# Sample attention in a hybrid decoder step: groups of four batches with small tiles, in place of pairs of batches with zero-filled queries

## The chip, the cores and the metric

One Trainium2 chip, of which the kernel uses one core. The metric is the device time of one execution in microseconds (us). A core has a tensor engine (TensorE, PE in the profile, its weight loads PEld), VectorE (DVE), ScalarE (ACT), GpSimd (POOL) and SyncE (SP), whose queue issues most DMA transfers. Each engine runs its instructions in the order in which the program emits them, and waits on semaphores of others.

## The reference

The kernel is one layer of a decoder trunk for two groups of requests: one prompt of 1024 tokens, and eight decode batches ("samples") of 8 new tokens each over 4096 past tokens in a paged cache. Per layer:

```python
h = rms_norm(x) * (1 + scale1) + shift1
z = h @ w_in                              # split among three mixers A, B, C
# A: 8 query heads, 2 key heads, 64 wide. Three branches, mixed by gates:
k_cmp, v_cmp = compress(raw keys), compress(raw values)     # 255 blocks of 32 tokens, stride 16
o_cmp, p     = cmp_attention(q, k_cmp, v_cmp)
top_i, ok    = select_blocks(p, ...)                        # 16 blocks of 64 tokens, per key head and token
o_slc        = slc_attention(q, top_i, ok, k_slc, v_slc)
o_win        = window attention over the last 512 tokens
mix_A        = g0 * o_cmp + g1 * o_slc + g2 * o_win
# B: gated convolution, C: pooling
x = x + gate1 * (concat[A, B, C] @ w_out)
x = x + gate2 * SwiGLU(rms_norm(x) * (1 + scale2) + shift2)
```

A query head r = 0..3 of key group g attends with key head g. For a sample batch that makes 4 heads × 8 tokens = 32 rows per key group, and 64 rows for both.

## The kernel before

The program is one long Python function that emits instructions. Its parts are tasks (generators), each of which emits a step and then yields the time from which its next step can run. A rough clock of the engines (`use`), priorities (`spawn`), conditions (`hold`) and lists of free PSUM banks by tag (`bank_of`, `give`) decide which task emits next. What comes out is a fixed order for each engine; nothing is reordered on the chip by these times. All products go through the helper at L135, transposes through L139, evictions through L150 (ACT) and L152 (DVE), so those lines stand for many sources, and tiles tell them apart.

The stages of the profiled execution: the conditioning up to about 110 us, the input projection up to about 380, the attention from 401 to 843, then the output projection and the feed-forward network. In the attention three tasks are interleaved on PE: the prompt's attention (tiles `kh`, `kl`, `qs`, `pt`, `vt`, `vcp`), the compression of the cached raw keys and values of batches 3 to 7 (tile `stream` from `cacheA`), and the sample attention, which this change is about.

The sample attention before works in four pairs of batches. Rows of a PSUM bank are (batch of the pair, key group, head, token) = 2·2·4·8 = 128. All 128 partitions of a key tile hold both key heads, 64 features each, so the query tile `qb` has 64 columns for a batch and zeros where a row's key group isn't the partition's (`sample_setup`, L1065).

- `sample_select` (L1081) runs once a pair, after both batches are compressed: scores against the 255 compressed blocks and the 16 new keys, softmax, the importance of 64-token blocks, the 16 best by two `max` and `match_replace` steps, a bias per block, and the values of these branches.
- `sample_attention` (L1198) then walks nine units a pair, 36 in all. A unit is 512 keys of each of the two batches, eight pages of 128 KB (`unit` or `stream` tiles, key half and value half): eight units of the cache and one of the window. Two products against the unit's keys fill the bank S, one 64-column tile of PE for each batch:

```python
for b2 in range(2):
    self.mm(S[self.rows(b2), 0:512], self.qb[:, 2 * p + b2], kv[:, b2, :, 0:P], True, True)
```

- DVE adds the bias and takes the row's extreme (L1225), ACT exponentiates (L1232).
- `sample_values` (L1238): four transposes of the 128×512 probabilities `e`, an eviction to `spt`, and eight products of 128 columns, four key tiles for two batches:

```python
for t in range(4):
    for b2 in range(2):
        self.mm(o[self.rows(b2), 0:P], pt[:, t * P + 64 * b2:t * P + 64 * b2 + 64],
                kv[:, b2, t, P:2 * P], t == 0, t == 3)
```

The half of the 128 result columns that belongs to the other key group is not used.

- `sample_load` and `sample_fetch` (L1176, L1187) load the next unit as soon as a buffer is free. There are two `unit` buffers, and three `stream` buffers more when all eight batches are compressed. SyncE issues a unit's eight pages one after the other (L488). A unit's scores wait in emission for `u in self.loads and self.u_done >= u - 1`.
- `sample_combine` (L1260) weighs the 12 partial results `part` of a pair by their maxima and sums and stores the mixture, which the output projection loads.

Constants made before (`constants3`, L293 to L328): `m_new` masks the new keys, `sel` picks a row's gates, `hind` its head, `rsum` sums the heads.

Of the kernel before, what the change touches and what calls it, by code (L numbers as in the profile page):

```python
# [7 lines left out]
F32 = mybir.dt.float32  # L8
# [4 lines left out]
OP = mybir.AluOpType  # L13
# [4 lines left out]
P = 128  # L18
# [42 lines left out]
class Kernel:  # L61
# [55 lines left out]
    def bank_of(self, tag):  # L117
        """waits for a bank of the tag"""
# [4 lines left out]
    # ---------------------------------------------------------------- helpers  # L123
# [22 lines left out]
    def evac(self, out, in_, n, ready=None):  # L146
        """PSUM to SBUF on the engine that is free first; the time at which it is there"""
# [7 lines left out]
    def combine(self, out, a, b, op, n, ready=0.0, eng=None):  # L155
        """out = a op b in SBUF on VectorE or GpSimd, by default the one that is done first"""
# [25 lines left out]
    # ---------------------------------------------------------------- constants  # L182
# [60 lines left out]
    def constants3(self, c):  # L243
        nc = self.nc
        with self.pool("ctmp") as tp:
# [9 lines left out]
            # zeros, then the causal triangle; the window's older edge; the compressed blocks that are not over yet  # L255
# [15 lines left out]
            # row index -> token t of a sample row (b2, g, r, t)  # L271
# [7 lines left out]
            # sum over the four heads of a key group  # L279
# [12 lines left out]
            # new tokens: key (b', t') is seen by row (b, t) when b' == b and t' <= t  # L292
            a = tp.tile([P, 4, 64], F32, name="a")  # L293
            for b2 in range(2):
                nc.gpsimd.iota(a[64 * b2:64 * b2 + 64], pattern=[[-16, 4], [1, 64]], base=-8 * b2,
                               channel_multiplier=0, allow_small_or_imprecise_dtypes=True)
            ge = tp.tile([P, 4, 64], F32, name="ge")
            nc.vector.tensor_scalar(ge, a, 0.0, None, op0=OP.is_ge)
            ok = tp.tile([P, 4, 64], F32, name="ok")
            nc.vector.scalar_tensor_tensor(ok, a, tv[:, 0:1], ge, op0=OP.is_le, op1=OP.mult)  # L300
            self.m_new = c.tile([P, 4, 64], F32, name="m_new")
# [9 lines left out]
            # token partition (64 + (b, t)) -> row (b2, g, r, t) of the pair p  # L311
            self.sel = c.tile([P, 4, P], F32, name="sel")
            si = tp.tile([P, 4, 2, 8, 8], F32, name="si")
            for p in range(4):
                nc.gpsimd.iota(si[:, p], pattern=[[-8, 2], [0, 8], [-1, 8]], base=-64 - 16 * p,
                               channel_multiplier=1, allow_small_or_imprecise_dtypes=True)
            nc.vector.tensor_scalar(self.sel.rearrange("a p r -> a (p r)"), si.rearrange("a p b g t -> a (p b g t)"),
                                    0.0, None, op0=OP.is_equal)

            # head of a sample row  # L320
            hi = tp.tile([P, 8], F32, name="hi")
            for b2 in range(2):
                nc.gpsimd.iota(hi[64 * b2:64 * b2 + 64], pattern=[[-8, 8]], base=0, channel_multiplier=1,
                               allow_small_or_imprecise_dtypes=True)
# [1810 lines left out]
```

## Time and profile before

| | us |
|---|---|
| three runs | 1708.04, 1712.49, 1713.70 |
| median | 1712.49 |
| span of the profiled execution | 1707.9 |
| PE busy in it | 1606.5 (94%) |
| DVE, ACT, POOL busy | 1121.0, 821.8, 704.6 |

The span is the time from the first to the last instruction of the one execution that was profiled. That execution has no device time of its own beside its span; the nearest figure is the span's distance of 4.6 us to the runs' median. In the rows of a view, `L135 PE MATMUL bank<-unit,qb 128*64 128x512 f32 x4` is: line, engine, instruction, what is written from which tiles (moving operand, then weights), the tile of PE as rows*columns, the moving operand's partitions × columns, and the number of records. A product of fp32 operands leaves two records, one for each pass.

### The profile page before, as it was taken

What the parts mean: (1) busy time and instruction counts of PE and PEld (TensorE: products, weight loads), DVE (VectorE), ACT (ScalarE), POOL (GpSimd) and SP (SyncE); (2) the same over time, 40 slices, a digit from 0 to 9 for tenths busy, and PEclk for the clock granted to TensorE, in tenths of its full rate; (3) what the DMA queues carried; (4) which work ended last, traced back from release to release, by engine and by line L of the source; (5) the groups of instructions that cost most, each with busy time, mean ns of one, the idle gap of its engine ahead of it and who ended that gap; (6) DMA issues with size and microseconds to landing.
All of it is one profiled execution on the core that took longest, in us unless ns stands there. A gap on an engine that the chain in (4) does not pass through costs nothing.

```text
span 1707.9 us, 35277 instructions
## 1 busy us (share of the span) xinstructions
PE 1606.5 (94%) x12317; PEld 1427.7 (84%) x12317; DVE 1121.0 (66%) x2886; ACT 821.8 (48%) x1892; POOL 704.6 (41%) x812
## 2 busy tenths in 40 slices
PE   6789999997999999999799789999999999899998
PEld 5689999987877566666599779999999998889997
DVE  1491334767556867666599996555555556998887
ACT  1363212326676766766675543332333334655554
POOL 1121000003342322222206486555555555888976
PEclk9899999999999999999999989999999999999999
DMA  9854455425664644540883224225222225744433
GB/s 273 258 180 127 143 141 138 136 75 179 202 193 128 195 141 122 160 131 10 276 253 105 75 72 135 96 96 194 97 96 100 96 96 186 237 128 130 133 82 125
DMA packets 214851, 245.13 MB, mean 144 GB/s; under 512 B 25985, under 2 KB 182850, under 8 KB 214354
## 3 DMA queue, kind: packets, MB, share of 16 engines
q1 hardware_dynamic: 190546, 209.77, 40.1%
q10 hardware_dynamic: 18288, 17.01, 3.2%
q0 software_dynamic: 5840, 16.10, 2.9%
q8 instruction: 98, 1.61, 0.4%
q14 instruction: 79, 0.65, 0.1%
HBM read 202.33 MB, written 44.67 MB: 145 GB/s over the span
## 4 chain that ended last, share of the span: by engine, by line
PE 31%; DVE 9%; issue 4%; DMA 3%; POOL 3%; ACT 1%; ACTq 0%; POOLq 0%; DVEq 0%; SPq 0%
PE bank L135 31%; DVE w_lo L160 2%; DMA w_raw<-in_wup 2%; POOL w_s L160 1%; DVE b_lo L160 1%; DVE g_lo L160 1%; DVE x L1706 1%; DVE d_lo L160 1%; POOL b_t L160 1%; DMA w_raw<-in_wdown 0%; DMA mixc<-mix_d 0%; ACT w_hi L164 0%; DMA x<-x_d 0%; DVE n_ss L160 0%; POOL f_T L160 0%
## 5 line engine op out<-in xcount | busy, mean ns | idle before, releaser
L135 PE MATMUL bank<-b_lo,w_hi 128*128 128x272 f32 x1232 | 355.8, 291 | 2.7 <-DVE b_lo L160 2.5
L135 PE MATMUL bank<-b_hi,w_hi 128*128 128x272 f32 x1232 | 351.6, 292 | 6.9 <-DVE f_v L1512 3.3
L135 PE MATMUL bank<-b_hi,w_lo 128*128 128x272 f32 x1232 | 351.4, 290 | 2.1 <-DVE w_lo L160 2.1
L135 PEld LDWEIGHTS bank<-b_hi,w_hi 128*128 128x128 f32 x1232 | 232.1, 191 | 9.6 <-ACT b_hi L164 4.9
L135 PEld LDWEIGHTS bank<-b_lo,w_hi 128*128 128x128 f32 x1232 | 234.5, 190 | 4.0 <-DVE b_lo L160 3.9
L135 PEld LDWEIGHTS bank<-b_hi,w_lo 128*128 128x128 f32 x1232 | 233.0, 190 | 3.1 <-DVE w_lo L160 2.8
L160 POOL TENSOR_TENSOR w_s<-w_raw 128x512 f32<-128x512 f32 (+1 forms) x122 | 164.2, 1347 | 147.8 <-DVE w_lo L160 134.1
L1011 POOL TENSOR_SCALAR P<-P,st 128x640 f32<-128x640 f32 (+11 forms) x192 | 111.5, 591 | 241.8 <-DVE st L1009 89.5
L164 ACT ACTIVATE w_hi<-w_raw 128x512 fp32r<-128x512 f32 (+2 forms) x130 | 86.5, 676 | 176.5 <-PE bank L135 141.2
L160 DVE TENSOR_TENSOR w_lo<-w_raw,w_hi 128x512 fp32r<-128x512 f32 (+2 forms) x129 | 115.6, 904 | 83.2 <-PE bank L135 47.4
L160 DVE TENSOR_TENSOR w_lo<-w_s,w_hi 128x512 fp32r<-128x512 f32 (+1 forms) x144 | 127.4, 888 | 45.4 <-ACT w_hi L164 38.6
L135 PE MATMUL bank<-stream 128*128 128x128 f32 x1056 | 137.2, 289 | 19.4 <-DMA stream<-in_cacheA 14.5
L135 PEld LDWEIGHTS bank<-stream 128*128 128x128 f32 x1056 | 130.4, 203 | 28.5 <-issue 21.8
L160 POOL TENSOR_TENSOR x<-x,d_m 128x272 f32<-128x272 f32 x144 | 141.1, 1001 | 25.2 <-DVE x L1706 13.1
L164 ACT ACTIVATE w_hi<-w_s 128x512 fp32r<-128x512 f32 (+1 forms) x144 | 89.2, 624 | 113.2 <-PE bank L135 57.1
L135 PE MATMUL bank<-h_hi,w_hi 128*128 128x384 f32 (+1 forms) x384 | 129.4, 337 | 1.0 <-ACT py L826 1.0
L135 PE MATMUL bank<-h_hi,w_lo 128*128 128x384 f32 (+1 forms) x384 | 126.7, 330 | 0.0
L135 PE MATMUL bank<-h_lo,w_hi 128*128 128x384 f32 (+1 forms) x384 | 126.4, 329 | 0.0
L1003 ACT ACTIVATE P<-P,st 128x640 f32<-128x640 f32 (+11 forms) x192 | 113.0, 591 | 13.0 <-DVE st L994 6.5
L135 PE MATMUL bank<-g_hi,w_hi 128*128 128x272 f32 x308 | 92.0, 301 | 13.1 <-DVE x L1706 6.7
L139 PEld LDWEIGHTS bank<-ident,P 128*128 128x128 f32 (+1 forms) x592 | 64.1, 138 | 46.4 <-issue 30.2
L139 PE MATMUL bank<-ident,P 128*128 128x128 f32 (+1 forms) x592 | 95.6, 284 | 2.5 <-DVE pt L152 1.7
(363 smaller groups left out, 4111.0 us busy)
## 6 DMA issues: line engine op xcount, KB each, us to landing
wada<-in_wada SPq DMA_DIRECT2D x96, 256.0 KB, 5.2
stream<-in_cacheA SPq DMA_DIRECT2D x192, 128.0 KB, 3.1
w_raw<-in_wup SPq DMA_DIRECT2D x48, 512.0 KB, 3.9
g_raw<-g_d SPq DMA_DIRECT2D x70, 272.0 KB, 3.1
unit<-in_cacheB SPq DMA_DIRECT2D x136, 128.0 KB, 2.3
stream<-in_cacheB SPq DMA_DIRECT2D x120, 128.0 KB, 2.2
w_raw<-in_wout SPq DMA_DIRECT2D x24, 512.0 KB, 4.5
g_d<-f_T SPq DMA_DIRECT2D x84, 136.0 KB, 1.8
```

The costliest lines, as they stand in the source:

```text
L135: self.nc.tensor.matmul(out, lhsT, rhs, start=start, stop=stop, skip_group_check=chain)
L139: self.nc.tensor.transpose(out, in_, self.ident)
L160: (self.nc.vector if eng == "dve" else self.nc.gpsimd).tensor_tensor(out, a, b, op=op)
L164: self.nc.scalar.activation(hi, src, AF.Copy)
L1003: nc.scalar.activation(Ps, Ps, AF.Exp, scale=-1.0, bias=sy[:, 0:1], accum_out=sy[:, 1:2])
L1011: nc.gpsimd.tensor_scalar(Ps, Ps, sy[:, 3:4], 0.0, op0=OP.mult, op1=OP.add)
L1706: nc.vector.scalar_tensor_tensor(out[:, :n], acc[:, :n], self.mod[:, 5, m, 0:1], out[:, :n], op0=OP.mult, op1=OP.add)
```

## The change

The sample attention works in two groups Q of four batches. Rows of a bank are (batch, head, token) = 4·4·8 = 128 for one key group, and there is a bank, a bias, a probability tile and so on for each of the two key groups. `qb` has 32 columns and no zeros: partitions 0 to 63 hold the queries of key group 0, the others those of group 1. Scores are products of tiles with 64 rows (a key group's features) and 32 columns (a batch's rows), eight for a step at eight places of the PE array. A value product has 32 columns of weights and 64 moving columns (a key group's values alone), four batches at four column places, 32 products a step. A step takes two of the units of before, and there are 18. `sample_select` runs once a group, waits for four batches, and loads keys and values of the blocks as separate halves.

```diff
 def sample_setup(self, pool):
-        self.qb = pool.tile([P, NB, 64], F32, name="qb")
-        nc.vector.memset(self.qb, 0.0)
-        for g in range(2):
-            s = slice(64 * g, 64 * g + 64)
-            nc.vector.tensor_copy(
-                self.qb[s].rearrange("p b (g r t) -> p g b r t", g=2, r=4)[:, g],
-                self.q[s, :, SEQ:].rearrange("p r (b t) -> p b r t", t=NT))
+        self.qb = pool.tile([P, NB, 32], F32, name="qb")
+        nc.vector.tensor_copy(self.qb.rearrange("p b (r t) -> p b r t", r=4),
+                              self.q[:, :, SEQ:].rearrange("p r (b t) -> p b r t", t=NT))
...
-    def rows(self, b2):
-        return slice(64 * b2, 64 * b2 + 64)
+    def rows(self, b):
+        return slice(32 * b, 32 * b + 32)
+    def group(self, g):
+        return slice(64 * g, 64 * g + 64)
+    def sample_scores(self, S, col, Q, keys):
+        for b in range(4):
+            for g in range(2):
+                k = keys(b)[self.group(g)]
+                n = 1
+                for d in k.shape[1:]:
+                    n *= d
+                self.mm(S[g][self.rows(b), col:col + n], self.qb[self.group(g), 4 * Q + b], k, True, True)
...
 def sample_select(self, pool, Q, st):
-        yield from self.hold(lambda: self.cmp_done >= 2 * p + 2)
-        for b2 in range(2):
-            t = pool.tile([P, 2, 256], F32, name="kvc", bufs=2)
-            nc.sync.dma_start(t, self.cmp_d[2 * p + b2])
-            kv.append(t)
+        yield from self.hold(lambda: self.cmp_done >= 4 * Q + 4)
+        def load(x):
+            t = [pool.tile([P, 2, P], F32, name="kvc", bufs=4) for b in range(4)]
+            for b in range(4):
+                nc.sync.dma_start(t[b], self.cmp_d[4 * Q + b][:, :, x * P:(x + 1) * P])
+            return t, self.use("dma", 1.5, self.t["pe"]) + 2.5
+        K, at = load(0)
...
+        self.sample_scores(S, 0, Q, lambda b: K[b])
+        self.sample_scores(S, 256, Q, lambda b: self.kn)
+        V, at = load(1)
+        for g in range(2):
...
+            for h in range(2):
+                n = P if h == 0 else NCMP - P
+                for b in range(4):
+                    self.mm(o[self.rows(b), 0:64], ct[:n, h, self.rows(b)], V[b][:n, h, self.group(g)], h == 0, h == 1)
...
 def sample_fetch(self, u, kv):
-        p, x = divmod(u, 9)
+        Q, x, c = u // 18, u % 18 // 2, u % 2
...
 def sample_attention(self, pool):
-        for u in range(36):
+        for Q in range(2):
+            self.spawn(1, self.sample_select(pool, Q, sts[Q]))
+        for u in range(18):
...
-            yield from self.hold(lambda: "at" in st and u in self.loads and self.u_done >= u - 1)
+            yield from self.hold(lambda: "at" in st and 2 * u + 1 in self.loads and self.u_done >= 2 * u - 2)
+            kv, at, src = zip(*[self.loads.pop(2 * u + c) for c in range(2)])
...
-            S = yield from self.bank_of("S")
-            for b2 in range(2):
-                self.mm(S[self.rows(b2), 0:512], self.qb[:, 2 * p + b2], kv[:, b2, :, 0:P], True, True)
+            S = []
+            for g in range(2):
+                S.append((yield from self.bank_of("S")))
+            self.sample_scores(S, 0, Q, lambda b: kv[b // 2][:, b % 2, :, 0:P])
...
 def sample_values(self, pool, u, st, kv, es, nx, src):
...
-        for t in range(4):
-            for b2 in range(2):
-                self.mm(o[self.rows(b2), 0:P], pt[:, t * P + 64 * b2:t * P + 64 * b2 + 64], kv[:, b2, t, P:2 * P],
-                        t == 0, t == 3)
+        for g in range(2):
+            for t in range(4):
+                for b in range(4):
+                    self.mm(o[self.rows(b), self.group(g)], pts[g][:, t * P + 32 * b:t * P + 32 * b + 32],
+                            kv[b // 2][:, b % 2, t, P + 64 * g:P + 64 * g + 64], t == 0, t == 3)
...
-        self.unit_free.append(src)
+        self.unit_free += src
         self.sample_load(pool)
-        self.u_done += 1
+        self.u_done += 2
```

`sample_combine` does the same sums for two key groups of half the width (two combines, 24 wide operations each, for four with 12), with one transpose and one copy each, and stores 32 tokens at a time (two stores for four). The masks in `constants3` are laid out by the new rows. The other lines of the diff take out comments.

More of the change, by code (lines that the diff above doesn't have):

```diff
@@ L1204, in sample_attention @@
         self.sample_load(pool)
[L1205 to L1220 removed]
+        sts = [{} for _ in range(2)]
@@ new lines, in sample_attention @@
+        for Q in range(2):
+            self.spawn(1, self.sample_select(pool, Q, sts[Q]))
+        for u in range(18):
+            Q, x = divmod(u, 9)
+            st = sts[Q]
+            yield from self.hold(lambda: "at" in st and 2 * u + 1 in self.loads and self.u_done >= 2 * u - 2)
+            kv, at, src = zip(*[self.loads.pop(2 * u + c) for c in range(2)])
+            yield max(*at, st["at"])
+            S = []
+            for g in range(2):
+                S.append((yield from self.bank_of("S")))
+            self.sample_scores(S, 0, Q, lambda b: kv[b // 2][:, b % 2, :, 0:P])
@@ L1230, in sample_attention @@
[L1230 to L1245 removed]
+            es = []
@@ new lines, in sample_attention, with sample_values @@
+            self.spawn(2, self.sample_values(pool, u, st, kv, es, nx, src))
+            yield 0.0
+    def sample_values(self, pool, u, st, kv, es, nx, src):
+        pts = []
+        for e, ready in es:
+            yield ready
+            tr = yield from self.bank_of("t")
+            for t in range(4):
+                self.tr(tr[:, t * P:(t + 1) * P], e[:, t * P:(t + 1) * P])
+            pt = pool.tile([P, 512], F32, name="spt", bufs=2)
+            r = self.evac(pt, tr, 512)
+            self.give("t", r)
+            pts.append(pt)
@@ new lines, in sample_combine @@
+        o = pool.tile([P, 2, 64], F32, name="co", bufs=2)
+        for g in range(2):
+            nc.vector.tensor_scalar(o[:, g], part[:, 11, g], gr[:, g, 0:1], None, op0=OP.mult)
+            for c in range(11):
+                nc.vector.scalar_tensor_tensor(o[:, g], part[:, c, g], w[:, g, c:c + 1], o[:, g], op0=OP.mult, op1=OP.add)
+        yield self.use("dve", 6.5, self.t["pe"]) + 0.5
+        tr = yield from self.bank_of("t")
+        self.tr(tr[:, 0:P], o.rearrange("p g d -> p (g d)"))
```

286 lines of the change are left out of this document (125 added, 161 removed).

## The prediction

> **What bounds the kernel now.** I read the page's head and its 40 slices first, then one window of the sample attention, then what PE waited for in it, then single timelines for prices. The order of PE's instructions, and its counts, I took from the two compiled programs.
>
> ```profile
> span 1707.9 us, 35277 instructions
> PE 1606.5 (94%) x12317; PEld 1427.7 (84%) x12317; DVE 1121.0 (66%) x2886; ACT 821.8 (48%) x1892; POOL 704.6 (41%) x812
> ...
> PE   6789999997999999999799789999999999899998
> PEclk9899999999999999999999989999999999999999
> ```
> ```profile
> core 0: us, PE busy (x) PEld busy (x) DVE busy (x) ACT busy (x) POOL busy (x), PEclk, DMA share, GB/s
> 401.00:843.00 442.00, 423.55 (x3200) 286.38 (x3199) 288.43 (x1399) 302.82 (x795) 132.09 (x229) 0.99 0.51 157
> ```
> ```profile
> PE bank L135 <- ACT w_hi L164: 6.2, 1, 6.2
> PE bank L135 <- DVE pre L544: 1.9, 1, 1.9
> PE bank L139 <- DVE pt L152: 1.7, 2, 0.9
> PE bank L135 <- ACT ksq L594: 1.6, 1, 1.6
> ...
> PE bank L135 <- DMA unit<-in_cacheB: 0.7, 2, 0.5
> ```
>
> The slices show PE at 9 tenths nearly throughout, at full granted clock. The window from 401 to 843 us is the stage in which all sample attention lies, interleaved on PE with the prompt's attention and the compression; PE is busy for 423.6 of 442 us, while DVE has 288 and ACT 303. The waits (columns: us in total, times, longest) are small: 6.2 us once at the hand-over to the output projection, under 2 us each else, and 0.7 us for the selection's pages. So PE's own instructions set this stage, and the change is worth what it does to PE's time there, less new waits.
>
> **Prices from the rows.** The first timeline is one unit of the selection before the change: columns are start, us, instruction, count.
>
> ```profile
> 762.85 1.09 PE L135 MATMUL bank<-stream,spt 128*64 128x128 f32 x16
> 763.77 1.03 PE L135 MATMUL bank<-unit,qb 128*64 128x512 f32 x4
> 764.73 0.66 PE L139 MATMUL bank<-ident,e 128*128 128x128 f32 x4
> 765.32 0.65 PE L135 MATMUL bank<-pt,vt__610 128*64 128x256 f32 x4
> 765.80 1.03 PE L135 MATMUL bank<-stream,qb 128*64 128x512 f32 x4
> 766.76 0.51 PE L135 MATMUL bank<-kh,qs 128*128 128x512 f32 x1
> ```
> ```profile
> 212.76 1.08 PE L135 MATMUL bank<-wada,sc 128*32 128x128 f32 x32
> 213.77 0.44 PE L135 MATMUL bank<-h_hi,w_hi 128*128 128x384 f32 x1
> ```
> ```profile
> 444.52 0.66 PE L135 MATMUL bank<-vt,c_w 64*64 64x256 f32 x8 [0.43 <-ACT vt L579]
> 445.11 0.40 PE L135 MATMUL bank<-gates,sel 128*128 128x24 f32 x2
> 445.36 0.41 PE L135 MATMUL bank<-i,rsum 128*128 128x64 f32 x2
> ```
>
> Starts are observed and ends modelled, so I price by the distance between starts. Every fp32 product leaves two records (two passes). Sixteen value records on two column tiles of 64 take 763.77 − 762.85 = 0.92 us: eight side-by-side passes of 128 columns, with some 0.05 us for the first weights, so 0.109 us a pass. A score group, two products side by side, takes 764.73 − 763.77 = 0.96: two passes of 512 columns at 0.43 = 0.86, and 0.10 left; the tile shape changes behind it from 128*64 to 128*128, and I call the 0.09 to 0.10 the drain at a change of shape. The `wada,sc` row shows four column tiles of 32 side by side: 32 records in 213.77 − 212.76 = 1.01 us, eight passes of four at 0.109 plus a change. The `vt,c_w` row does the same for four quarters of 64*64: 8 records in 0.59, two passes of four at 0.22, plus change and weights. So both shapes of the changed kernel have a relative that runs four abreast at full streaming rate. Eight tiles of 64*32 at once appear in no row.
>
> **The change, part by part.** Counts are those of the compiled orders; "stretch" means products of one kind with nothing else between.
>
> *Scores.* Before, 72 products stand in 33 stretches: 24 of one unit's two, 5 of two units' four, 4 of a single one. A column position is used once per 0.86 us, so this is 24×0.86 + 5×1.72 + 4×0.86 = 32.7 us. After, each step has eight products on eight different positions, which could all pass in one 0.86: 18×0.86 = 15.5, a saving of 17. But the compiled order cuts the 144 products into 44 stretches (28 of two, 8 of four, 4 of six, 4 of eight) with prompt or compression products between, in none of which a position repeats. A stretch costs 0.86 with two tiles or with eight: 44×0.86 = 37.8, that is +5.1. If products on free positions ran beside a whole-array product, this would be lower; the 0.96 of the quoted groups gives no sign of it.
>
> *Values.* Before, 288 products, 149 side-by-side places of two passes of 128 columns: 149×0.218 = 32.5. After, 576 products in fours of 64 columns; counting for each stretch its most used position gives 161 places. A pass of 64 columns at half of 0.109 is an estimate of 0.055, two passes 0.111: 161×0.111 = 17.9, so −14.6. The nearest row against it is `gates,sel`: two records with only 24 columns take 445.36 − 445.11 = 0.25 us, so a 128-wide weight load sets some 0.11 to 0.12; a load a quarter as wide, four abreast, would stay below 0.055, and `wada,sc` loads four 32-wide weights per 0.109 without loss. Bounds: 17.9 at the streaming rate, and 31.1 at the fastest rate that a row holds for a whole stretch (32 records in 8×0.109 us, 27 ns a record, 64 records in a step: 18×64×0.027).
>
> ```profile
> L135 PE MATMUL bank<-unit,qb 128*64 128x512 f32 x76 | 22.0, 607 | 0.6 <-DMA unit<-in_cacheB 0.5
> L135 PE MATMUL bank<-stream,qb 128*64 128x512 f32 x68 | 17.6, 607 | 0.0
> L135 PE MATMUL bank<-unit,spt 128*64 128x128 f32 x304 | 21.9, 280 | 1.1 <-DVE vcT L596 1.1
> L135 PE MATMUL bank<-stream,spt 128*64 128x128 f32 x272 | 20.5, 280 | 0.0
> L135 PE MATMUL bank<-kvc,qb 128*64 128x256 f32 x16 | 3.1, 392 | 0.0
> L135 PE MATMUL bank<-vt__610,ct 64*64 64x128 f32 x32 | 3.0, 283 | 0.0
> L135 PE MATMUL bank<-kvc,ct 128*64 128x128 f32 x16 | 2.2, 295 | 0.0
> ```
>
> These groups confirm the counts (76 + 68 = 144 score records, 304 + 272 = 576 value records); their busy sums hold modelled ends, so they lie above my sums.
>
> *Select.* Per pair: compressed scores 0.44, new-key scores 0.22, the two value parts 0.44 each; 1.53 × 4 pairs = 6.1. After, the same per group of four: 1.53 × 2 = 3.1. −3.0. The gate and sum products, and the transposes, keep their number.
>
> *Changes of shape.* 410 in this stage before, 460 after; 50×0.092 = +4.6.
>
> *Loads.* A step now needs two units and frees two buffers together; before it was one by one, over the same five buffers.
>
> ```profile
> 469.38 4.32 SPq L488 DMA_DIRECT2D unit<-in_cacheB  x8
> ```
> ```profile
> DMA to landing us min/median/max: 2.0/2.3/5.2
> ```
>
> SyncE takes 4.32 us to issue a unit's eight pages, the last of which lands 2.3 later: 6.6 us from a free buffer, and 10.9 for the second unit of a pair freed at once (4.32 + 4.32 + 2.3). By the compiled order the PE work between a buffer's last value product and the first score product of its next load is under 9 us in 3 of 34 cases before (5.3, 5.7, 5.7), which cost the 0.7 us quoted, and in 13 of 34 after (4.0, 5.1, 6.1, 6.2, 6.7, 7.5, then 8.0 to 8.9). Against 6.6 the shortfalls of the first four add to 5.0; against 10.9 all thirteen add to 48. The first unit of a freed pair is needed one step before the second, so I take +3, nearer to the lower end; bounds 1 (the same under-cost as the three cases before) and 48. Behind a waiting score product everything on PE waits, prompt products too.
>
> *Other waits.* +1 for a select that now needs four batches' blocks before it starts and an extra loading of the value half (16 loads of half size for 8, on SyncE's queue before the next pages); bounds −1 and +4, two waits as long as the largest quoted beside the hand-over (1.9).
>
> *At nothing.* Softmax, exponentials and the evictions of the probabilities keep their number and size on DVE and ACT, part evictions fall from 36 to 18, the combine has the same 44 multiply-adds at half the width; with 288 and 303 of 442 us busy neither engine is on the path, and if that cover failed only the last combine could show. After it the order has prompt work alone, some 39 us on PE (27 before). The setup's copies and masks lie before 401. The hand-over stays:
>
> ```profile
> 836.17 0.65 PE L135 MATMUL bank<-pt,vcp 63*64 63x256 f32 x4 [0.16 <-ACT pt L150]
> 842.97 0.60 PE L135 MATMUL bank<-mh,w_hi 128*128 128x272 f32 x1 [6.15 <-ACT w_hi L164]
> ```
>
> This 6.15 us hangs on the end of the prompt's keys, which lies as far ahead of the first output product as before (188 products for 183).
>
> *Sum.* +5.1 − 14.6 − 3.0 + 4.6 = −7.9, waits +3 +1: **−3.9 us**. The profiled span is 1707.9, 4.6 below the median of the runs (1712.5); the same distance kept, span 1704.0 and **1708.6 us**. A measurement of this kernel tells 0.3%, 5.1 us, from no change, so this is inside "same".
>
> **The rivals.**
>
> *No new waits, faster.* The priced sum holds and the loads stay ahead of PE, as 31 of 34 did before. −7.9, to −12 if fragments cost less than whole passes: about 1704.6. For it: DMA share 0.51 in the window. Chance 0.22.
>
> *Issue limit, slower.* Value products get so short that PE's front sets the time. No row holds a pace above a record per 27 ns over a whole stretch; at that pace values cost 31.1 instead of 17.9, +13.2 on the forecast: +9.3, 1721.8. It turns the sign from 19 ns a record, where the 1152 records cost 21.8, 3.9 more than at the streaming rate. Against it:
>
> ```profile
> 212.76 0.32 PE L135 MATMUL bank<-wada,sc 128*32 128x128 f32 x4
> ```
> ```profile
> 212.76 0.16 PEld L135 LDWEIGHTS bank<-wada,sc 128*32 128x32 f32 x8 [0.19 <-PE bank L135]
> ```
>
> Cut at 212.79 the timeline holds four products begun, cut at 212.82 eight weight loads: twelve instructions in 0.06 us, 5 ns each, where a four of values needs eight in 0.055. That is a burst, the pace over 64 records is open. Chance 0.17. The Trainium skill has such a floor ("TensorE: Matmul & The Clock Gate", section "Wait — 56ns, not 53.3ns?"): starts of products never come closer than about 25 ns however small the product; by it a step's 64 records would take an estimated 1.6 us and all values 28.8, which is +7.0 and 1719.5. The burst of four speaks against it as a rule for products on different column tiles.
>
> *Loads in pairs, slower.* The thirteen short reuses wait for the second unit. A third of the upper bound, 16, on −7.9 is +8.1: 1720.6. It decides once load waits pass 7.9 us in all. For it: with 4.32 us of issue a unit, two freed at once queue behind each other and behind the compression's pages. Against: only one of the thirteen distances is below 5 us, and prompt work between is re-orderable only by the program, not by the chip. Chance 0.19.
>
> That the change doesn't do what it says can be left out: the compiled order holds the new tiles.
>
> **How the numbers follow.** Forecast 0.42; with its waits between their bounds of 0 and +8 it spans −7.9 to 0, a third of it (0.14) beyond −5.1. Faster: 0.22 + 0.14 = 0.36. Same: 0.28. Slower: 0.17 + 0.19 = 0.36. The forecast's own range is 1704 to 1713. The whole range reaches down to 1701 (the gain with cheap fragments) and up to 1725, which takes in both slower centres with 3 us more of waits, and leaves out the paired loads' upper part.
>
> **What would show it.** In the profile after: value fours at 0.11 a place (32 products unbroken in some 0.9 us; 1.7 would be the issue limit); a score stretch of two as long as one of eight, 0.86; the score group's mean count per stretch; PE's waits for unit loads at 1 to 5 us (over 8: paired loads); window 401 to the hand-over shorter by 4. Wrong if DVE or ACT turn up as releasers of PE for over 5 us, if eight 64*32 tiles take over 0.86, or if the hand-over's 6.15 us moves.

## The result, and the profile after

The changed kernel takes 1728.6 us (median of four runs, 1725.4 to 1734.5) against 1710.9 for the kernel before: a ratio of 1.0102, 95% interval [1.0081, 1.0123]. It is slower by 1%; the forecast was a gain of 0.2%, and the stated range ended at 1725. The profiled span grew from 1707.9 to 1724.4, by 16.5 us.

The page after, its first lines:

```profile
span 1724.4 us, 36881 instructions
PE 1610.5 (93%) x13131; PEld 1415.7 (82%) x13131; DVE 1106.3 (64%) x2854; ACT 817.9 (47%) x1880; POOL 704.7 (41%) x818
```

Of the 16.5 us, 15.9 lie in the attention. From the first product with the prompt's keys to the first of the output projection it took 442.3 us before and 458.2 after (the stages ahead of and behind it agree within 2 us). I cut this stretch once more, at the last compression product on the tile `stream`. Windows of the kernel before, then of the changed one:

```profile
400.70:537.50 136.80, 129.93 (x1037) 103.99 (x1037) 80.27 (x415) 92.77 (x267) 47.67 (x104) 0.99 0.64 197
537.50:843.00 305.50, 293.92 (x2168) 182.69 (x2166) 208.46 (x984) 210.12 (x528) 84.42 (x125) 1.00 0.45 139
```
```profile
401.90:535.00 133.10, 118.44 (x1042) 99.19 (x1041) 72.12 (x376) 83.74 (x238) 44.31 (x96) 0.95 0.60 179
535.00:860.20 325.20, 309.97 (x2978) 175.80 (x2977) 206.51 (x990) 215.96 (x545) 88.99 (x133) 1.00 0.47 141
```

The columns are the length, then PE, PEld, DVE, ACT and POOL busy, the granted clock, the DMA share and GB/s. PE's idle time is the length less PE's busy time: 6.9 and 11.6 before, 14.7 and 15.2 after. The clock column gives a second loss: 118.44 us at 0.95 is some 6 us of lost pulses, 129.93 at 0.99 is 1.3. For the table further down I summed both finer (idle from the union of PE's records, clock in windows of about 4 us), which splits each attention stage into **work at full clock, idle and clock loss**:

| | attention | work | idle | clock loss |
|---|---|---|---|---|
| before | 442.3 | 422.3 | 18.5 | 1.5 |
| after | 458.2 | 422.3 | 29.9 | 6.1 |

So the products were not cheaper in sum, PE idled 11.4 us more, and the clock took 4.6 more. Of these last two, 7.8 and 4.6 lie before the last compression product. Each split is of the one profiled execution of a kernel. PE's waits in the attention after:

```profile
PE bank L135 <- DMA stream<-in_cacheA: 5.8, 3, 3.0
PE bank L135 <- ACT w_hi L164: 5.1, 1, 5.1
PE bank L135 <- DVE pt L152: 3.0, 1, 3.0
PE bank L139 <- DVE pt L152: 3.0, 4, 1.5
PE bank L135 <- DMA stream<-in_cacheB: 2.0, 1, 2.0
PE bank L135 <- DMA unit<-in_cacheB: 1.5, 3, 0.9
```

The raw pages (`cacheA`) of the compression lead the list; the selection's pages (`cacheB`) take 3.5 in all, for 0.7. Before, the raw pages cost PE this much:

```profile
PE bank L135 <- DMA stream<-in_cacheA: 0.3, 1, 0.3
```

Summed by what ended them, the 11.4 us of additional idle time are 5.5 for raw pages, 2.8 for the selection's pages, 2.6 for DVE (7.8 for 5.2), 0.5 for ACT and GpSimd, 1.1 in which no releaser shows, and 1.1 less at the hand-over. PE at 419 to 438 us of the changed kernel:

```profile
419.06 0.66 PE L139 MATMUL bank<-ident,P 128*128 128x128 f32 x4
422.69 6.20 PE L135 MATMUL bank<-stream 128*128 128x128 f32 x32 [2.98 <-DMA stream<-in_cacheA]
428.82 0.65 PE L135 MATMUL bank<-pt,vt__610 128*64 128x256 f32 x4
429.40 0.77 PE L139 MATMUL bank<-ident,P 128*128 128x128 f32 x5
430.01 3.74 PE L135 MATMUL bank<-stream 128*128 128x128 f32 x32
...
436.73 1.57 PE L135 MATMUL bank<-stream 128*128 128x128 f32 x11 [2.00 <-DMA stream<-in_cacheA]
```

Behind a wait of 2.98 us the 32 products took 6.20 us, with a granted clock of 0.50 from 420.9 to 427.7; the next 32, without a wait, took 3.74. In the kernel before, products of the first pair's select (`kvc`, `kn`) stand between the same groups:

```profile
411.50 0.65 PE L135 MATMUL bank<-kvc,qb 128*64 128x256 f32 x4
411.99 0.39 PE L135 MATMUL bank<-kn,qb 128*64 128x128 f32 x4
...
423.00 3.74 PE L135 MATMUL bank<-stream 128*128 128x128 f32 x32
426.67 0.43 PE L135 MATMUL bank<-kvc,ct 128*64 128x128 f32 x2
427.03 3.84 PE L135 MATMUL bank<-stream 128*128 128x128 f32 x32
430.80 0.66 PE L135 MATMUL bank<-kvc,ct 127*64 127x128 f32 x6
```

The first of these groups began at 423.00 before and at 422.69 after, so PE came to it no later; it had less to do ahead of it, since the select now waits for a fourth batch.

The prices of the tiles came out as predicted. A whole step's scores and a whole step's values, in one piece each:

```profile
482.12 1.09 PE L135 MATMUL bank<-unit,qb 64*32 64x512 f32 x16
483.14 0.70 PE L135 MATMUL bank<-ksq,mean_h 128*128 128x256 f32 x2
...
502.81 1.10 PE L135 MATMUL bank<-unit,spt 128*32 128x64 f32 x64
503.84 0.65 PE L135 MATMUL bank<-pt,vcp 15*64 15x256 f32 x4
```

Eight tiles at once take 483.14 − 482.12 = 1.02 us, 64 value records 1.03, change of shape included. But most steps look like this one:

```profile
655.90 1.05 PE L135 MATMUL bank<-unit,qb 64*32 64x512 f32 x4
656.88 0.65 PE L135 MATMUL bank<-pt,vt__610 128*64 128x256 f32 x4
657.46 0.66 PE L139 MATMUL bank<-ident,P 128*128 128x128 f32 x4
658.05 1.05 PE L135 MATMUL bank<-unit,qb 64*32 64x512 f32 x4
659.03 0.48 PE L135 MATMUL bank<-kh,qs 128*128 128x448 f32 x1
659.35 0.37 PE L135 MATMUL bank<-kl,qs 128*128 128x448 f32 x1
659.64 1.06 PE L135 MATMUL bank<-unit,qb 64*32 64x512 f32 x8
```

Two products, a batch's two key groups, take 656.88 − 655.90 = 0.98 us, nearly as long as eight. The program emits all eight together, with nothing between, so PE's order is not simply that of emission: the framework's planner, which orders each engine by a simulated timeline, places a batch's two as soon as its pages are due, some 2 us apart. Summing starts to next starts over the attention, without the longer waits: scores 36.0 → 46.1 us, values 37.8 → 24.3, the select's products 9.3 → 6.1.

The hand-over to the output projection is as before:

```profile
854.41 0.65 PE L135 MATMUL bank<-pt,vcp 63*64 63x256 f32 x4 [0.16 <-ACT pt L150]
860.19 0.59 PE L135 MATMUL bank<-mh,w_hi 128*128 128x272 f32 x1 [5.13 <-ACT w_hi L164]
```

### The profile page after: what moved, and what is told of

It reads as the page before. It is cut to its first block, busy times and chain, and to the rows that moved or that the text cites. A ratio compares the mean times of both kernels' runs of the same rounds, so it can differ in the third digit from the quotient of the medians.

```text
span 1724.4 us, 36881 instructions
## 1 busy us (share of the span) xinstructions
PE 1610.5 (93%) x13131; PEld 1415.7 (82%) x13131; DVE 1106.3 (64%) x2854; ACT 817.9 (47%) x1880; POOL 704.7 (41%) x818
## 5 line engine op out<-in xcount | busy, mean ns | idle before, releaser
L1011 POOL TENSOR_SCALAR P<-P,st 128x640 f32<-128x640 f32 (+11 forms) x192 | 112.6, 596 | 265.4 <-DVE st L1009 97.0
L135 PE MATMUL bank<-stream 128*128 128x128 f32 x1056 | 143.4, 299 | 26.7 <-DMA stream<-in_cacheA 19.3
L135 PEld LDWEIGHTS bank<-stream 128*128 128x128 f32 x1056 | 137.4, 212 | 34.4 <-issue 24.4
L1003 ACT ACTIVATE P<-P,st 128x640 f32<-128x640 f32 (+11 forms) x192 | 113.1, 590 | 27.8 <-DVE st L994 15.3
L135 PE MATMUL bank<-g_hi,w_hi 128*128 128x272 f32 x308 | 90.5, 296 | 16.5 <-DVE x L1723 11.1
```

Of the source, the lines that this page charges most:

```text
L135: self.nc.tensor.matmul(out, lhsT, rhs, start=start, stop=stop, skip_group_check=chain)
L1003: nc.scalar.activation(Ps, Ps, AF.Exp, scale=-1.0, bias=sy[:, 0:1], accum_out=sy[:, 1:2])
L1011: nc.gpsimd.tensor_scalar(Ps, Ps, sy[:, 3:4], 0.0, op0=OP.mult, op1=OP.add)
```

## The experiments

Each ratio is against runs of the kernel before on the same chip. The table gives all of them with the split of their attention stage in us; the edits follow. "Held" means that the eight scores of a step are ordered together, "shared" that GpSimd issues part of the pages, "four early" that four batches in place of three are compressed beside the input projection. The split is of one execution, which lay up to 7.5 us above the median of its kernel's runs (1722.7 for 1715.2 with steps 4 us later, 1724.8 for 1718.3 with raw pages shared), so small differences of medians can't be read from it.

| kernel | median, us | ratio to before, 95% interval | attention | work | idle | clock loss |
|---|---|---|---|---|---|---|
| kernel before, select waits for four | 1735.7 | 1.0123 [1.0094, 1.0153] | 463.7 | 420.5 | 32.3 | 10.7 |
| kernel before, four batches early | 1713.4 | 1.0012 [0.9994, 1.0031] | 437.0 | 406.2 | 21.1 | 9.8 |
| kernel before, unit pages shared | 1720.4 | 1.0067 [1.0041, 1.0093] | 444.5 | 419.3 | 22.3 | 2.6 |
| changed, first units loaded late | 1731.7 | 1.0095 [1.0067, 1.0123] | 462.6 | 423.0 | 29.2 | 10.4 |
| changed, select loads on GpSimd | 1728.1 | 1.0078 [1.0050, 1.0105] | 457.6 | 423.5 | 29.6 | 4.4 |
| changed, four batches early | 1727.2 | 1.0091 [1.0062, 1.0120] | 447.4 | 403.4 | 33.9 | 10.0 |
| changed, scores held | 1735.1 | 1.0125 [1.0096, 1.0153] | 468.9 | 399.5 | 53.6 | 15.8 |
| changed, unit pages shared | 1730.9 | 1.0111 [1.0083, 1.0139] | 460.2 | 416.9 | 36.0 | 7.4 |
| changed, raw pages shared | 1718.3 | 1.0042 [1.0026, 1.0058] | 455.8 | 411.9 | 32.0 | 11.9 |
| changed, half steps | 1729.1 | 1.0093 [1.0070, 1.0116] | 456.1 | 405.8 | 37.1 | 13.2 |
| changed, half steps, held | 1732.4 | 1.0110 [1.0086, 1.0133] | 461.8 | 399.2 | 42.7 | 19.7 |
| changed, held, unit pages shared | 1720.5 | 1.0042 [1.0021, 1.0063] | 450.1 | 396.2 | 44.6 | 9.3 |
| changed, held, unit pages shared, four early | 1723.6 | 1.0077 [1.0049, 1.0104] | 441.0 | 376.8 | 54.4 | 9.7 |
| changed, held, both shared | 1716.2 | 1.0027 [1.0010, 1.0045] | 447.0 | 397.3 | 37.0 | 12.7 |
| changed, held, raw pages shared | 1726.0 | 1.0077 [1.0049, 1.0105] | 462.5 | 394.9 | 52.2 | 15.3 |
| the same, steps 4 us later | 1718.8 | 1.0026 [1.0007, 1.0046] | 455.3 | 396.1 | 46.0 | 13.3 |
| changed, steps 4 us later | 1715.2 | 1.0022 [0.9998, 1.0046] | 449.3 | 408.2 | 32.9 | 8.1 |
| **changed, steps 8 us later** | **1703.3** | **0.9971 [0.9956, 0.9987]** | 433.9 | 396.7 | 29.0 | 8.3 |

**The late select alone, in the kernel before.**

```diff
-        yield from self.hold(lambda: self.cmp_done >= 2 * p + 2)
+        yield from self.hold(lambda: self.cmp_done >= 4 * (p // 2) + 4)
```

> The kernel before, with one edit: a pair's select waits until the whole group of four batches is compressed. Tiles, counts and loads stay as before. Early-filler theory (after the change PE idled 2.98 and 2.0 us for compression pages at 420 and 435, because the select that used to lie there waits for a fourth batch, and the granted clock fell to 0.78): 8 to 13 us slower than before, with waits for the compression's pages near 420 and a clock dip. Cut-scores theory (44 stretches of scores at 0.98 each are what costs): no change, within 3 us.

It lost 23.1 us, more than the whole change and more than the 8 to 13 expected, with the old tiles and a work sum that did not grow. Its waits up to the last compression product, and the window:

```profile
PE bank L135 <- DMA stream<-in_cacheA: 6.6, 3, 4.6
PE bank L135 <- ACT vt L579: 5.8, 3, 5.3
PE bank L135 <- DMA kvc<-cmp_d: 2.7, 1, 2.7
```
```profile
405.40:561.60 156.20, 135.78 (x1039) 108.78 (x1037) 79.99 (x412) 90.77 (x265) 47.60 (x104) 0.92 0.58 173
```

Idle there is 20.4 us (6.9 before) and the clock 0.92. Waiting for a group of four is enough to make a loss of this size in the kernel before, though only 6.6 of the 20.4 us were spent on raw pages. The changed kernel shows the same signs in the same place, smaller.

**The first units' pages later, and the select's loads on another queue.**

```diff
         self.unit_next = 0
-        self.sample_load(pool)
...
+        yield from self.hold(lambda: self.cmp_done >= 4)
+        self.sample_load(pool)
```

> The changed kernel, with the first two units' sixteen pages issued only after the fourth batch is compressed; they lie ahead of the compression's pages on SyncE's queue for some 10 us at 405. Early-filler theory: the pages come up to 10 us earlier, the waits of 2.98 and 2.0 at 420 and 435 and the clock dip go: 4 to 10 us faster than the changed kernel (1728.6). Cut-scores theory: within 2 us of it.

```diff
-                nc.sync.dma_start(t[b], self.cmp_d[4 * Q + b][:, :, x * P:(x + 1) * P])
+                nc.gpsimd.dma_start(t[b], self.cmp_d[4 * Q + b][:, :, x * P:(x + 1) * P])
```

> The changed kernel, with the select's sixteen loads of compressed blocks issued by GpSimd's queue in place of SyncE's. Queue theory (these loads wait for the fourth batch and for the score products, and hold back the compression's pages behind them on SyncE, which stood idle from 445.8 to 452.7): 4 to 8 us faster than 1728.6. Cut-scores and early-filler theories: within 2 us of 1728.6.

Neither gained. With the late pages, idle before the last compression product did fall, from 14.7 to 9.5, but behind it idle rose from 15.2 to 19.7, and 4.4 us of clock were lost there, where none had been. The queue theory falls with the second.

**Four batches compressed early**, as a control in the kernel before and in the changed one.

```diff
-EARLY = 3
+EARLY = 4
```

> The kernel before, with four batches' blocks compressed beside the input projection in place of three; the attention then compresses four. A control for the next run: the 16 us that late select lost in the kernel before came from an empty stretch near 440, which this kernel doesn't have, so by the early-filler theory it moves by at most 4 us either way (the moved compression is PE work in both places); if a fourth batch in the projection costs by itself, it is slower by over 4.

> The changed kernel, with four batches compressed beside the input projection, so that the first group's select can run at the start of the attention. Early-filler theory: before the compression's end the changed kernel lost 14.7 us idle and 6.1 us of clock, against 6.9 and 1.5; those 12 us come back: 1714 to 1718. Its rival, that the loads in pairs of units cost the time in any place: within 4 us of 1728.6.

This did not settle it. The control moved by 2.3 us, within its 4. The changed kernel gained 1.4 us, not the 11 to 15 of the early-filler theory, and lies in the range of the rival; ahead of the last compression product it still idled 14.6 us and lost 5.6 of clock, though its first select could run at once. But the control lost more there too, 9.4 and 8.3 for 6.9 and 1.5, since the compression that moved into the projection, 12 to 13 us of it, was filler itself. The attention became shorter by 5.3 us in the kernel before and by 10.8 in the changed one, so the early filler is worth at most the difference of some 5 us by this route.

**The eight scores held together.**

```diff
+        first = None
-        for b in range(4):
-            for g in range(2):
+        for b in (3, 0, 1, 2):
+            for g in (1, 0):
...
+                with ExitStack() as s:
+                    if first is not None:
+                        s.enter_context(self.tc.issue_after(first.ins))
+                    m = self.mm(S[g][self.rows(b), col:col + n], self.qb[self.group(g), 4 * Q + b], k, True, True)
+                    first = first or m
```

> The changed kernel, with the eight score products of a step held together: the first emitted is the one whose page lands last, and the other seven are ordered behind it. Stretches of scores fall from 44 to 20, changes of tile shape from 460 to 426. Cut-scores theory: 24 stretches at 0.98 are 23 us less, so 1705 to 1710, faster than the kernel before. Early-filler theory: the early loss stays, and by it alone the time stays within 3 us of 1728.6; both together would give some 1705 with the waits before 470 unchanged. If the scores now wait for the last page with nothing beside them, up to half of the 23 comes back as waits for unit and stream pages.

Work fell by 22.8 us, about what 24 stretches at 0.98 cost. The time did not fall with it, 1735.1 against 1728.6: idle grew by 23.7 and the clock loss by 9.7. PE's waits, and the window behind the last compression product:

```profile
PE bank L135 <- DMA stream<-in_cacheA: 11.4, 4, 4.3
PE bank L135 <- DMA stream<-in_cacheB: 7.9, 4, 4.4
PE bank L135 <- DMA unit<-in_cacheB: 6.3, 5, 1.6
```
```profile
537.90:871.10 333.20, 295.82 (x2978) 179.31 (x2976) 208.45 (x990) 215.08 (x545) 88.30 (x133) 0.96 0.46 138
```

The selection's pages went from 3.5 to 14.2 us, and 333.20 − 295.82 = 37.4 us are idle. A first product that waits for the last page holds all of PE's queue.

**Half steps**: a step of one unit with 256 keys of each of four batches, so that each buffer is freed and refilled by itself. The edit replaces the step's loop; its core:

```diff
-        for u in range(18):
-            Q, x = divmod(u, 9)
+        for u in range(36):
+            Q, x = divmod(u, 18)
...
-            yield from self.hold(lambda: "at" in st and 2 * u + 1 in self.loads and self.u_done >= 2 * u - 2)
+            yield from self.hold(lambda: "at" in st and u in self.loads and self.u_done >= u - 1)
```

> The changed kernel with steps of half the size: a step takes one unit, 256 keys of each of the four batches (two pages a batch) in place of two units with 512 keys, so a buffer is freed and refilled by itself as before the change, over the same five buffers; the tiles, the groups of four and the select stay. There are 36 steps with eight score products of 256 columns, twice as many bias, exponential and partial-sum operations of half the width, and 21 partial results in place of 12. Granularity theory (double steps that free two buffers at once make PE idle): idle in the attention falls from 29.9 towards the 18.5 of the kernel before, scores cost 55 stretches at 0.53 in place of 45 at 1.02: 1702 to 1714. Late-select theory (the group of four alone makes the loss, as it made 23 us in the kernel before): the idle before the compression's end stays at 14 us or more, and the time at 1715 to 1726.

> The same with the score products of a step ordered behind the one whose page lands last (47 stretches for 55). Granularity theory: 1700 to 1712, since a step now waits for one unit alone. If holding the scores together makes PE wait whatever the step's size, as it did with double steps (+6.5 us), it is 3 to 8 us slower than the run before it.

Work fell by 16.5 us in the first, but idle grew by 7.2 and clock loss by 7.1, and 1729.1 lies outside the ranges of both theories. The second was 3.3 us slower, at the edge of its 3 to 8 and no clear difference. Freeing the buffers one by one did not remove the idle time, which speaks against the granularity theory; since half steps also bring twice as many bias, exponential and partial-sum operations, this does not clear the pairs of buffers altogether.

**Page issue shared with GpSimd.** Unit pages two and two, raw pages five and three (of 8, before six and two):

```diff
-            at = self.gather(kv[:, 4 * b2:4 * b2 + 4], "cacheB", 4 * Q + 2 * c + b2, 4 * x, 4)
+            at = self.gather(kv[:, 4 * b2:4 * b2 + 4], "cacheB", 4 * Q + 2 * c + b2, 4 * x, 4, 2)
```
```diff
-            self.raw[i] = (t, self.gather(t, "cacheA", i // 4, i % 4 * 8, 8, 2))
+            self.raw[i] = (t, self.gather(t, "cacheA", i // 4, i % 4 * 8, 8, 3))
```

> The changed kernel; GpSimd issues two of a batch's four pages of a unit, SyncE the others. Pace theory: the stretch from the first key product to the last compression product is paced by SyncE's queue (133 us for 20 octets of pages, 6.6 us each, with 112.4 us of PE work in it); with fewer unit pages on that queue it shrinks to 110 to 122 us, as in the run with held scores (111), idle and clock loss in it fall from 20.8 to under 12, and the time to 1715 to 1721. If the idle comes from the change's own steps: within 4 us of 1728.6.

> The changed kernel; GpSimd issues three of the eight raw pages of a compression octet in place of two, the unit pages stay on SyncE. Pace theory: SyncE issues five pages for six, an octet takes up to a sixth less, the stretch shrinks from 133 to 113 to 125 us, and the time falls by 4 to 10 us. If the pace is not SyncE's: within 4 us of 1728.6.

> The kernel before, with the same sharing of unit pages as y2. It idled 18.5 us in the attention, 6.9 of it up to the last compression product, so by the pace theory it has little to gain: 1706 to 1713. If the sharing is a gain by itself, of the size seen with held scores (15 us), it is 1695 to 1704.

The pace theory was half right. With shared unit pages the stretch up to the last compression product did shrink, from 133.1 to 112.6:

```profile
402.30:514.90 112.60, 103.81 (x924) 89.61 (x923) 62.91 (x321) 75.28 (x207) 42.12 (x92) 0.95 0.63 192
514.90:862.50 347.60, 320.47 (x3095) 184.54 (x3094) 225.24 (x1047) 225.64 (x575) 158.64 (x265) 0.99 0.45 139
```

The time stayed, outside the 1715 to 1721 expected: of the 20.5 us by which the stretch shrank, 12.8 were work that moved behind it, and idle time behind it rose from 15.2 to 27.2. That the stretch shrank fits a pace set by SyncE's queue, but does not show it alone, since each edit also changes the planner's order: with held scores and both kinds of pages shared (below) the stretch took 148.6 us, with 127.6 of work in it.

Shared raw pages gained 10 us in the median, the upper end of what the theory gave. In the profiled execution the attention is only 2.4 us shorter: work is 10.4 less (that order has 41 stretches of scores and 430 changes of shape, for 44 and 460, but the scores took 45.6 us, nearly as long as before the edit), idle and clock loss 7.9 more. What made its work smaller was not separated. The kernel before lost 8.8 us by shared unit pages, outside both of its ranges, so the sharing is no gain by itself.

**Held scores with shared pages**, in four mixes:

> The run with the eight scores held together, with one more edit: GpSimd issues two of a batch's four pages of a unit, so that a pair of units is issued in about half of the 8.6 us. With the scores held together PE's work was 399.5 us at full clock, 23 less than in the changed kernel, but it idled 53.6 us, 16 of it for pages of the cache. Load-pace theory (freed pairs are refilled too slowly): idle falls by 10 to 20 us and the clock loss with it, 1712 to 1724. If the order of the steps and not the pace of the loads makes the waits: within 4 us of 1735.1.

> The changed kernel with all three: four batches compressed early, the eight scores held together, pages issued by two queues. If early filler and load pace are the two causes, their gains add: 1700 to 1708, faster than the kernel before. If either fails, 1712 to 1725.

> The changed kernel with held scores, unit pages shared two and two, raw pages five and three. Pace theory: against the run with held scores and shared unit pages (1720.5) another 3 to 8 us, 1712 to 1718, and faster than the kernel before only if the waits behind the compression's end (26.9 us idle there) fall as well. If pages no longer pace it: within 4 us of 1720.5.

> The changed kernel with held scores (20 stretches) and three of eight raw pages issued by GpSimd; unit pages stay on SyncE. If the gains add, held scores' 23 us of work and the 10 us that the shared raw pages gave: 1712 to 1720. If the waits of the held scores (54 us idle, 16 clock) stay: 1722 to 1730.

Held scores with shared unit pages gained 15 us over held scores alone, as the load-pace theory had it, with 9 us less idle. The best, with both shared, reached its 1712 to 1718 and is 0.27% slower than the kernel before. In the other two the gains did not add: 1723.6 and 1726.0 lie in the ranges given for that. None gets its work (377 to 397 us) into time: 37 to 54 us idle remain.

**The steps later in PE's order.** The last theory: the scores stand in PE's order as soon as their pages are due, piece by piece. Moving a step back in emission lets all its pages land, so that the planner finds the eight ready together, with other work placed ahead.

```diff
-            yield max(*at, st["at"])
+            yield max(*at, st["at"]) + 4.0
```

> The changed kernel, with each step of the sample attention emitted 4 us later by the rough clock after its pages are due, so that prompt products stand ahead of it in PE's order. The order has 31 stretches of scores for 44 and 427 changes of tile shape for 460. Early-order theory: the scores no longer wait for pages, work falls by 13 stretches (13 us), idle doesn't grow: 1712 to 1720. If work that is saved comes back as idle as in the other versions: within 4 us of 1728.6.

> The run before it, with the steps emitted 4 us later as well. Early-order theory: the held scores' waits for pages (16 us with held scores alone) shrink to under 5 and the time to 1700 to 1711, under the kernel before. Else within 4 us of the run before it.

> The changed kernel, with each step emitted 8 us later after its pages are due, in place of 4. Early-order theory: 5 stretches fewer, 5 us less work than with 4 us, idle before the last compression product as there: 1707 to 1713. If later steps now delay the refill of the buffers: 1716 to 1724.

For the changed kernel the theory's direction held, and most of its sizes. The orders have 44, 31 and 26 stretches of scores, the traces 46.1, 38.9 and 27.2 us for them, and the ratios to the kernel before are 1.0102, 1.0022 and 0.9971. With 4 us the work fell by 14.1 us (13 expected), while idle grew by 3.0 (none expected). With 8 us the time came below its range of 1707 to 1713, and the work fell by another 11.5 us, not 5: five stretches fewer are only part of it, since several stretches of the version with 4 us still take far longer than 1 us. On held scores with shared raw pages the delay gave 7 us, not the 15 and more expected, and the waits for the selection's pages stayed at 13.3 us, not under 5. The scores in PE's groups, changed kernel and then steps 8 us later:

```profile
L135 PE MATMUL bank<-stream,qb 64*32 64x512 f32 x144 | 28.2, 600 | 2.3 <-DMA stream<-in_cacheB 2.0 <-issue 0.2
L135 PE MATMUL bank<-unit,qb 64*32 64x512 f32 x144 | 23.3, 600 | 1.5 <-DMA unit<-in_cacheB 1.5
```
```profile
L135 PE MATMUL bank<-stream,qb 64*32 64x512 f32 x144 | 20.9, 600 | 0.0
L135 PE MATMUL bank<-unit,qb 64*32 64x512 f32 x144 | 14.2, 600 | 0.0
```

The same records, 51.5 and 35.1 us, and no wait for a page. The windows of that kernel:

```profile
400.10:530.90 130.80, 118.17 (x1050) 97.61 (x1049) 73.39 (x378) 84.28 (x239) 44.28 (x96) 0.96 0.61 182
530.90:834.10 303.20, 286.84 (x2970) 174.51 (x2968) 212.11 (x1001) 207.42 (x533) 87.99 (x133) 0.98 0.50 151
```

Behind the last compression product 286.84 us of PE against 309.97 in the changed kernel; ahead of it the loss stays, 12.6 us idle at a clock of 0.96. Of the 25.6 us of work that this version saves over the changed kernel, 18.9 are scores. Against the kernel before it saves as much work, of which 10.5 more idle and 6.8 more clock loss take back two thirds. It is faster than both kernels, though than the one before by 0.3% only. Whether the kernel before would gain by the same delay was not tried.

## Why the prediction was wrong, point by point

- **Prices of tiles: right.** Values were to save 14.6 us and saved 13.5, the select 3.0 and 3.2. The rival *issue limit* is refuted: 64 records in 1.03 us are 16 ns each, where it needed 27. The Trainium skill's floor ("TensorE: Matmul & The Clock Gate", section "Wait — 56ns, not 53.3ns?", starts no closer than about 25 ns) doesn't hold for products side by side on column tiles here; by it the 64 would have taken an estimated 1.6 us.
- **Scores: the term was mis-sized.** +5.1 was forecast, and one for the 11 additional changes of shape; +10.1 was measured. Three of the 45 stretches in the trace take 2.02, 2.25 and 1.56 us in place of about 1, which is 2.8 of the 4 us beyond the forecast; I take them for waits for pages, the loads' cost in another place, but only one of them shows an idle gap (0.22 us). I had counted the cut and priced it, but took it as given; it was what the change's worth hung on.
- **Sum of the work: −7.9 forecast, about 0 measured.** Scores explain 4, values 1. The rest, some 3 us, sits in products that the change doesn't touch; those with the prompt's keys (`kh`, `kl`) alone took 87.7 us for 84.9. It may hold dearer changes of shape, or waits that the modelled ends hide; this was not separated.
- **Waits: the step that failed.** "+1 for a select that now needs four batches' blocks": the same wait cost 23.1 us alone in the kernel before. The step named the loads and the queue, and not that the first pair's select was filler at 411 to 432 us, where PE otherwise waits for raw pages. No term of the sum stands for raw pages; they cost 5.5 us more. +4 was forecast for all waits, 11.4 us of idle time came.
- **The clock was put at nothing, without a reason.** The prediction read full granted clock from the slices and gave it no term; it took 4.6 us more, all of it ahead of the last compression product.
- **Loads in pairs: not decisive.** The selection's pages cost 3.5 us, 2.8 more than before, where +3 was forecast; the 7.9 at which this rival decides was not reached by waits that show. A slower outcome came, but not by this rival.
- **At nothing: right in the main.** The hand-over's wait moved by 1 us (5.13 for 6.15), and the tail behind the last combine was covered. PE's waits for ACT stayed (5.8 for 5.6, without the hand-over), but those for DVE grew to 7.8 us, over the 5 that the prediction named as a sign of being wrong; they were at 5.2 before the change already.

What stays open: in the changed kernel the loss ahead of the last compression product (14.7 idle and 6.1 clock, 6.9 and 1.5 before) was shown only by likeness to the kernel before with the late select. Early compression, which lets the first select run at once, left it in place (14.6 and 5.6), so the late select may not be all of it. No edit removed it: later loads, another queue and a faster pace left it, moved it or paid elsewhere.

## What to carry to other kernels

Tiles that run side by side pay only when they stand side by side in the engine's order: count the stretches, since two score tiles here cost nearly what eight cost (0.98 and 1.02 us). Where a planner places each product when its own data are due, a later start of the whole step can be worth more than an earlier one; an order edge to the last datum was no substitute here, since the queue waited with it. When a step is made to wait for more inputs, ask what it filled while the engine waited for something else.

## What the runs showed of the hardware

Short waits can cost more than their length, through the granted clock. In the changed kernel it was 0.50 for 6.8 us from the wait of 2.98 us on, and 32 products took 6.20 us where 3.74 is usual; behind 2.00 us it was 0.50 for 3.4 us. Behind 2.04 us at 590.7 us of the same trace it stayed at 1.00. Counted over the attention of all 20 traces, half clock began between the start of a wait and 2 us behind its end for 8 of 80 waits of 1.0 to 1.5 us, 16 of 51 of 1.5 to 2, 35 of 45 of 2 to 3, and 46 of 47 longer ones. The idle time in sum does not give the loss: 54.4 us went with 9.7 of clock loss in one version, 42.7 with 19.7 in another.

The Trainium skill ("TensorE: Matmul & The Clock Gate", section "Why this matters for your kernels") advises against gaps over about 3 us, after which the clock falls back. The traces agree in kind, but the clock fell behind shorter waits as well: 2.00 us here, and 1.60 us in the kernel before, where it was 0.50 from 416.9 to 420.3.

Eight tiles of 64*32 in two row groups and four column groups, which no row of the kernel before showed, run at once: 16 passes of 512 columns (eight products, two passes each) in 1.02 us, the change of shape included.
